# Up-projection tiles of two conv FFNs by seven block products on TensorE, with sums in place in PSUM

## Chip, core and metric

The program runs on one core of a Trainium2 chip. The metric is the device time of one execution in microseconds, where lower is better. All matrix products are made in three passes of float32r (a high and a low part of each operand), so that a product A·B is ah·bh + ah·bl + al·bh.

## What is computed

The reference is two layers of a diffusion backbone on 512 tokens of 1024 channels, with 256 tokens of context. Layer 0 is attention, layer 1 is Fourier mixing, and each ends with a gated feed-forward network with a depthwise convolution over three tokens. Cut to the part that the change touches:

```python
def conv_ffn(h, w_up, conv_w, conv_b, w_down):   # h: 512 x 1024, w_up: 1024 x 5632, w_down: 2816 x 1024
    u = h @ w_up                                  # gate and value, 2816 channels each
    u = depthwise_conv(u, conv_w) + conv_b        # taps at t-1, t, t+1, per channel
    gate, val = jnp.split(u, 2, axis=-1)
    return (silu(gate) * val) @ w_down
```

Around it stand RMS norms and adaLN: h = rms_norm(x) * (1 + scale) + shift, and x = x + gate * rms_norm(y). Scale, shift and gate come from products of the conditioning vector with 1024 x 6144 weights of each layer (the "adaLN sums" below).

## The kernel before

**Layout.** Channels are on partitions, tokens on the free axis: 8 channel tiles of x, 512 tokens, in two halves of 256. The modulated input of an FFN is held as `hh` and `hl` (high and low part, 8 x 512), the running output as `yT`.

**An FFN** (`ffn`, L974) works on 22 tiles `fi` of 128 gate channels and 128 value channels. For an ordinary tile the weights come by DMA (`raw`, 1 MB), are split into `wh` (a cast on ScalarE) and `wl` (a subtraction on VectorE), both by `split` at L113, and `up_mm` makes 8 x 3 matmuls of N=512 for the gate and as many for the value (`mm3`, L90 to L92). `conv` then takes the sums out of PSUM: one activation (L994) and two taps (L995, L997). `gated` makes silu (L1007), the product (L1008), and splits it into the pair `xh`, `xl`, the moving operand of the down-projection.

The first tiles (0 to 2, made of units u = 0 to 5) are different. They sweep over one half of the tokens while the other half's input is still being made (`begin`, `sweep`). In the second FFN the units' results still lack the tokens' norm factor R, which is multiplied in later at L993, with corrections of single columns (L1001). Meanwhile `remod` makes the real `hh` and `hl` (L216 to L223) for all later tiles.

**Groups.** `HALVES` splits the 22 tiles into 14 and 8. After a group its tiles are multiplied with their rows of `w_down` (`y_mm`), for 8 output tiles d. The first group's sums are copied to `yT` by ScalarE (L1100), the second's are added by VectorE (L1102). In the second group the first token half of all d goes first; then `mid` begins the next sub-layer for that half (norm sums at L170, R by L201, L204 and L205, the residual at L278 and L280, and for the Fourier part `hh` and `hl` at L332 and L333, squares summed by GpSimd at L339) while the second half's pass runs for d = 1 to 7. The squares of y of each half are summed by GpSimd (L253).

**Beside it.** The adaLN sums of layer 1 (`gemv_jobs`, L376 and L379, six jobs of five steps) run on VectorE in the first FFN, one step a tile and two an output tile of the first group (`GP = [1, 2]`).

**Order.** The tile framework schedules each engine's instructions into a fixed order at build time; an engine then works strictly in that order. Buffers come in rings: `raw` has three, `wh` and `wl` have four each, the accumulators `mm` have six banks of PSUM, `xh` and `xl` pairs (`Pairs`) have seven. SyncE issues the weight loads. `fence` and `held` keep some work behind other work.

## Time and profile before

| | us |
|---|---|
| Three runs | 1176.74, 1181.56, 1176.4 (median 1176.74) |
| Span of the profiled execution | 1176.5 |
| Busy: TensorE, VectorE, ScalarE, GpSimd | 1134.0, 751.6, 512.2, 201.1 |
| First FFN | about 340 to 703 |
| Fourier mixing | about 703 to 800 |
| Second FFN and the end | about 800 to 1176.5 |

The profile is taken from one execution. Its page gives busy times by engine, the chain of work that ended last and the costliest groups of instructions. Behind it the trace can be asked for groups by line and shape, for the table of windows, for the waits (an engine's idle time and who released it) and for the timeline. In a row of the timeline the first number is the start, the second the time until the last of its instructions ends, and brackets at the end give the idle time before it and its releaser. PE is TensorE (PEld its weight loads), DVE is VectorE, ACT is ScalarE, POOL is GpSimd. MATMUL ends are modelled and lie behind the start of the next; starts tell the pace.

### The profile page before, as it was taken

To read this page: it belongs to the slowest core of one execution; us is meant where nothing else is said; L and a number is where in the kernel's file an instruction comes from. 1 tells how busy PE (TensorE), PEld (TensorE's weight loads), DVE (VectorE), ACT (ScalarE), POOL (GpSimd) and SP (SyncE) were. 2 spreads that over 40 slices of the span, in tenths; PEclk is the share of its full clock that TensorE was granted. 3 is DMA by queue.
4 is the path that set the end of the run, shared out by engine and by line. 5 is a ranking of instruction groups with operands and counts; after the bars stand their busy time and mean duration, and the time that the engine had idled before them with its cause. 6 is when DMAs were issued, how large, how long until landed. Compare 5 with 4: busy or idle time off the path is not lost.

```text
span 1176.5 us, 17135 instructions
## 1 busy us (share of the span) xinstructions
PE 1134.0 (96%) x6878; PEld 946.1 (80%) x6878; DVE 751.6 (64%) x1215; ACT 512.2 (44%) x887; POOL 201.1 (17%) x213
## 2 busy tenths in 40 slices
PE   7999999999999999999999998988999999999995
PEld 4689898679898877777878998877788888888895
DVE  4673777675779685756665568988966532255555
ACT  3332356566554434322444445646644332234342
POOL 1132534222320000000000153663000000000013
PEclk9999999999999999999999999998999999999998
DMA  9432110874115353666622301621233222332112
GB/s 371 187 127 72 37 36 7 298 306 152 65 43 209 108 208 110 237 238 225 233 90 56 116 11 35 210 81 60 72 108 103 73 84 99 108 108 72 54 55 72
DMA packets 27127, 145.18 MB, mean 123 GB/s; under 512 B 2724, under 2 KB 7460, under 8 KB 14120
## 3 DMA queue, kind: packets, MB, share of 16 engines
q1 hardware_dynamic: 27048, 144.09, 35.0%
q8 instruction: 54, 0.88, 0.3%
q14 instruction: 25, 0.20, 0.1%
HBM read 141.98 MB, written 2.10 MB: 122 GB/s over the span
## 4 chain that ended last, share of the span: by engine, by line
PE 84%; DVE 11%; DMA 1%; ACT 1%; issue 1%; POOL 1%; SPq 0%; DVEq 0%; ACTq 0%; POOLq 0%
PE mm L90 24%; PE mm L92 23%; PE mm L91 23%; DVE md_t L278 2%; PE PT L786 2%; PE gm L405 1%; DVE hl L333 1%; PE O L90 1%; DVE wl L113 1%; DVE xT L280 1%; PE S L90 1%; PE O L91 1%; PE O L92 1%; PE S L92 1%; DMA xT<-in_xT 1%
## 5 line engine op out<-in xcount | busy, mean ns | idle before, releaser
L113 DVE TENSOR_TENSOR wl<-raw,wh 128x1024 fp32r<-128x1024 f32 (+1 forms) x139 | 167.6, 1210 | 207.8 <-ACT wh L113 207.5
L90 PE MATMUL mm<-hh,wh 128*128 128x512 f32 (+2 forms) x728 | 276.1, 379 | 0.0
L92 PE MATMUL mm<-hh,wl 128*128 128x512 f32 (+2 forms) x728 | 275.7, 379 | 0.0
L91 PE MATMUL mm<-hl,wh 128*128 128x512 f32 (+2 forms) x728 | 275.4, 378 | 0.0
L113 ACT CAST wh<-raw 128x1024 fp32r<-128x1024 f32 (+2 forms) x151 | 149.6, 999 | 183.4 <-PE mm L91 141.9
L90 PEld LDWEIGHTS mm<-hh,wh 128*128 128x128 f32 x728 | 137.7, 189 | 29.3 <-issue 1.2
L92 PEld LDWEIGHTS mm<-hh,wl 128*128 128x128 f32 x728 | 137.7, 189 | 27.9
L91 PEld LDWEIGHTS mm<-hl,wh 128*128 128x128 f32 x728 | 137.8, 189 | 27.5
L253 POOL TENSOR_TENSOR gacc<-gacc,sq 128x256 f32<-128x256 f32 (+1 forms) x35 | 31.5, 900 | 681.3 <-ACT sq L251 680.5
L90 PE MATMUL mm<-xh,wh 128*128 128x512 f32 (+1 forms) x368 | 131.5, 357 | 0.0
L91 PE MATMUL mm<-xl,wh 128*128 128x512 f32 (+1 forms) x368 | 130.6, 355 | 0.0
L92 PE MATMUL mm<-xh,wl 128*128 128x512 f32 (+1 forms) x368 | 130.5, 355 | 0.0
L90 PEld LDWEIGHTS mm<-xh,wh 128*128 128x128 f32 x368 | 69.2, 188 | 12.4 <-issue 1.2
L91 PEld LDWEIGHTS mm<-xl,wh 128*128 128x128 f32 x368 | 69.1, 188 | 11.1
L92 PEld LDWEIGHTS mm<-xh,wl 128*128 128x128 f32 x368 | 69.0, 187 | 11.0
L113 ACT CAST xh<-cv 128x512 fp32r<-128x512 f32 x44 | 27.3, 620 | 100.9 <-DVE cv L1008 100.9
L995 DVE SCALAR_TENSOR_TENSOR cv<-mm,cols,cv 128x511 f32<-128x511 f32 x83 | 61.8, 745 | 11.4 <-ACT cv L994 11.4
L994 ACT ACTIVATE cv<-mm,cols 128x512 f32<-128x512 f32 x83 | 64.2, 774 | 10.4 <-PE mm L92 10.4
L997 DVE SCALAR_TENSOR_TENSOR cv<-mm,cols,cv 128x511 f32<-128x511 f32 x83 | 62.2, 749 | 2.2
L1007 ACT ACTIVATE cv<-cv 128x512 f32<-128x512 f32 x44 | 27.8, 631 | 71.2 <-DVE cv L997 68.7
L379 DVE SCALAR_TENSOR_TENSOR gacc<-raw,scol,gacc 128x1024 f32<-128x1024 f32 x42 | 53.8, 1281 | 4.5 <-DMA raw<-in_mod_r 4.1
L91 PE MATMUL mm<-hl,xh 128*128 128x256 f32 (+1 forms) x160 | 47.3, 296 | 3.6 <-DVE hl L333 2.8
(358 smaller groups left out, 2238.7 us busy)
## 6 DMA issues: line engine op xcount, KB each, us to landing
raw<-in_w_up SPq DMA_DIRECT2D x44, 1024.0 KB, 5.0
raw<-in_mod_r SPq DMA_DIRECT2D x24, 1024.0 KB, 5.0
raw<-in_mod_p SPq DMA_DIRECT2D x16, 1024.0 KB, 6.4
raw<-in_w_down SPq DMA_DIRECT2D x16, 896.0 KB, 4.6
raw<-in_w_down SPq DMA_DIRECT2D x16, 512.0 KB, 3.7
raw<-in_w_in SPq DMA_DIRECT2D x6, 1024.0 KB, 5.0
raw<-in_w_out SPq DMA_DIRECT2D x4, 1024.0 KB, 6.0
raw<-in_w_f SPq DMA_DIRECT2D x8, 512.0 KB, 4.4
```

Of the source, the lines that this page charges most:

```text
L90: i = PE.matmul(out, lhsT=ah, rhs=bh, start=start, stop=False)
L91: PE.matmul(out, lhsT=ah, rhs=bl, start=False, stop=False)
L92: return i, PE.matmul(out, lhsT=al, rhs=bh, start=False, stop=stop)
L113: i = S.copy(out=h, in_=src), eng.tensor_tensor(out=l, in0=src, in1=f(h), op=ALU.subtract)
L253: G.tensor_tensor(out=self.acc[:, sl], in0=self.acc[:, sl], in1=sq[:, sl], op=ALU.add)
L278: m = V.scalar_tensor_tensor(out=t, in0=yT[:, k, hs], scalar=der[:, l, gi, k:k + 1], in1=R, op0=ALU.mult, op1=ALU.mult)
L379: held(V.scalar_tensor_tensor(out=acc, in0=w[:, i, :], scalar=scol[:, 0, k:k + 1], in1=acc, op0=ALU.mult, op1=ALU.add))
L786: PE.transpose(out=pt[:, j * P:(j + 1) * P], in_=Ps[j][:, off:off + P], identity=ident)
L994: S.activation(out=cv, in_=ps, func=AF.Identity, bias=bc, scale=wc[1])
L995: V.scalar_tensor_tensor(out=cv[:, 1:], in0=ps[:, :T - 1], scalar=wc[0], in1=cv[:, 1:], op0=ALU.mult, op1=ALU.add)
L997: V.scalar_tensor_tensor(out=cv[:, :T - 1], in0=ps[:, 1:], scalar=wc[2], in1=cv[:, :T - 1], op0=ALU.mult, op1=ALU.add)
L1007: S.activation(out=cg, in_=cg, func=AF.Silu)
```

## The change

In 6 tiles of the first FFN (4, 7, 10, 13, 16, 19) and 9 of the second (4, 6, ... 20) the up-projection is made by seven block products instead of eight. Channels are cut in two blocks of four tiles, tokens in two halves of 256, and the tile's outputs are gate and value: a 2 x 2 by 2 x 2 block product. Each of the seven is 4 x 3 matmuls of N=256.

- `seven_inputs`, once in each FFN, makes four sums of input blocks in `yT` on VectorE (L969 to L972) and splits them into four new pairs `zh`, `zl`. For this `remod` keeps the modulated float32 values in `yT`, with one more ScalarE operation for every second channel tile (`kept`).
- `seven_weights`, for each tile, makes four sums of weight blocks on VectorE (L984, L986, L987, in a buffer of the `raw` ring) and four splits: "1" of 512 columns, "57", "63" and "24" of 1024.
- `seven_products` uses two accumulators x and y. Sums of products that are needed in two places are copied by ScalarE (L1017, L1019, L1022, L1027, 128x256) and added by VectorE in place in PSUM (L1025, L1028, 128x512). The value comes out negated, so the convolution takes negated taps (`ncw`).
- The 22 tiles form three groups of 8, 8 and 6. Groups two and three are added to `yT` by VectorE. In every group the first two output tiles are begun with all but the last channel tile. `w_down` of a group comes in one split for each output tile.
- The ring of `wh` and `wl` has five buffers, the ring of `xh` and `xl` pairs four, beside the four `zh`, `zl`. In the last group output tiles 4 to 6 take theirs from `zh`, `zl`.
- The adaLN sums take one step at an ordinary tile, none at a seven-product tile, and one at an output tile of the first two groups. The last of the six jobs moves into the second FFN.

Line numbers of the changed kernel differ: `split` is L118, `mm3` is L95 to L97, the conv's lines are L1075 (product with R), L1076, L1077, L1079 and L1083, `gated` is L1089 and L1090, the remodulation L221 to L229, the adaLN step L390, the norm sums' matmuls L175 and L360, GpSimd's adds L263, L290 and L350, the group sums L1191 and L1193.

```diff
-HALVES = [(0, 14), (14, 8)]
+GROUPS = [(0, 8), (8, 8), (16, 6)]
+FIRST = 3
+SEVEN = [range(4, NF, 3), range(4, NF, 2)]
-GP = [1, 2]
+GP = [1, 1]
...
     def wpair(shape):
-        return mk(wp, shape, F32R, "wh", 4), mk(wp, shape, F32R, "wl", 4)
+        return mk(wp, shape, F32R, "wh", 5), mk(wp, shape, F32R, "wl", 5)
...
-    def mod_tiles(items, R):
+    def mod_tiles(items, R, kept=None):
         for i, (h, l, src, am, bm) in enumerate(items):
-            t = mk(cp, [P, HT], F32, "md_t", 4)
-            if i % 2:
+            t = mk(cp, [P, HT], F32, "md_t", 4) if kept is None else kept[i]
+            if kept is not None and i % 2 == 0:
+                V.scalar_tensor_tensor(out=t, in0=src, scalar=am, in1=R, op0=ALU.mult, op1=ALU.mult)
+                S.activation(out=t, in_=t, func=AF.Identity, bias=bm, scale=1.0)
+                S.copy(out=h, in_=t)
+                V.tensor_tensor(out=l, in0=t, in1=f(h), op=ALU.subtract)
+            elif i % 2:
...
+    def seven_inputs(xp):
+        (b11, b12), (b21, b22) = blocks_of(yT)
+        hi, lo = blocks_of(hh), blocks_of(hl)
+        V.tensor_tensor(out=b11, in0=b11, in1=b12, op=ALU.subtract)
+        V.tensor_tensor(out=b12, in0=b22, in1=b12, op=ALU.subtract)
+        V.scalar_tensor_tensor(out=b22, in0=b22, scalar=-1.0, in1=b11, op0=ALU.mult, op1=ALU.subtract)
+        V.scalar_tensor_tensor(out=b21, in0=b22, scalar=-1.0, in1=b21, op0=ALU.mult, op1=ALU.subtract)
+        b = {"1": (hi[0][0], lo[0][0]), "2": (hi[1][0], lo[1][0]), "3": (hi[1][1], lo[1][1])}
+        for n, src in (("5", b11), ("6", b22), ("4", b21), ("7", b12)):
+            b[n] = xp.spare([P, KH, HT])
+            split(*b[n], src)
+        return b
+
+    def seven_weights(l, fi):
+        r = raw([P, 2, KC, P], a["w_up"][l, fi])
+        s = mk(wp, [P, 4, KH, P], F32, "raw", 3)
+        a4 = r.rearrange("p i (c k) n -> p (i c) k n", c=2)
+        V.tensor_tensor(out=s[:, 0:2], in0=a4[:, 3::-3], in1=a4[:, 2].unsqueeze(1).to_broadcast([P, 2, KH, P]),
+                        op=ALU.add)
+        V.tensor_tensor(out=s[:, 2], in0=s[:, 0], in1=a4[:, 0], op=ALU.add)
+        V.tensor_tensor(out=s[:, 3], in0=s[:, 2], in1=a4[:, 1], op=ALU.add)
+        w = {}
+        for names, src in (("1", a4[:, 0:1]), ("57", s[:, 0:2]), ("63", s[:, 2:4]), ("24", a4[:, 1::2])):
+            wh, wl = wpair([P, len(names), KH, P])
+            split(wh, wl, src)
+            for i, n in enumerate(names):
+                w[n] = wh[:, i], wl[:, i]
+        return w
...
+        product("1", y, 1)
+        S.copy(out=xs[:, :HT], in_=y[:, HT:])
+        product("5", x, 1)
+        S.copy(out=ys[:, HT:], in_=x[:, HT:])
+        product("2", x, 0)
+        product("6", y, 1)
+        S.copy(out=xs[:, HT:], in_=y[:, HT:])
+        product("4", y, 0)
+        product("3", x, 1)
+        V.tensor_tensor(out=x, in0=x, in1=xs, op=ALU.add)
+        product("7", y, 1)
+        S.copy(out=ys[:, :HT], in_=y[:, HT:])
+        V.tensor_tensor(out=y, in0=y, in1=ys, op=ALU.add)
+        return x, y
...
-        for hf, (f0, nch) in enumerate(HALVES):
-            for fi in range(max(f0, 3), f0 + nch):
+        bs = seven_inputs(xp)
...
+        for gi, (f0, nch) in enumerate(GROUPS):
+            end = gi == len(GROUPS) - 1
+            for fi in range(max(f0, FIRST), f0 + nch):
+                if fi in SEVEN[l]:
+                    cc = [conv(fi, i, u, None, i == 1) for i, u in enumerate(seven_products(l, fi, pps, bs))]
...
-                if gem is not None:
+                if gem is not None and fi not in SEVEN[l]:
                     pump(gem, GP[0])
...
-                if hf == 0:
+                if gi == 0:
                     S.copy(out=yT[:, d, sl], in_=ps[:, sl])
                 else:
                     V.tensor_tensor(out=yT[:, d, sl], in0=yT[:, d, sl], in1=ps[:, sl], op=ALU.add)
+                if end:
                     ys.add(pps, yT[:, d, sl], hs)
...
-                 gemv_jobs([(1, v) for v in range(6)], pps))
+                 gemv_jobs([(1, v) for v in range(5)], pps))
...
-                 lambda y: pump(boundary(y, 0, 1, 3, pps, None, a["out"]), 100), None, plain)
+                 lambda y: pump(boundary(y, 0, 1, 3, pps, None, a["out"]), 100), gemv_jobs([(1, 5)], pps), plain)
```

**VectorE, second FFN, around the beginning of tile 4.** Before, the convs of tiles 2 (cv of mm_1202), 3 (mm_1268, mm_1272) and 4 (mm_1277) stand here, with the split of tile 5's value weights (wl_1291) and the gates' splits (xl):

```order
L995 SCALAR_TENSOR_TENSOR cv1_1262_8183<-mm_1202_7739,cols_1_61,cv1_1262_8183 128x511
L113 TENSOR_TENSOR wl_1291_8375<-raw_1285_8339,wh_1290_8374 128x1024
L113 TENSOR_TENSOR xl_1255_8101<-cv1_1258_8113,xh_1254_8100 128x512
L997 SCALAR_TENSOR_TENSOR cv1_1262_8183<-mm_1202_7739,cols_1_61,cv1_1262_8183 128x511
L995 SCALAR_TENSOR_TENSOR cv0_1269_8224<-mm_1268_8199,cols_1_61,cv0_1269_8224 128x511
L1008 TENSOR_TENSOR cv1_1262_8183<-cv0_1260_8126,cv1_1262_8183 128x512
L997 SCALAR_TENSOR_TENSOR cv0_1269_8224<-mm_1268_8199,cols_1_61,cv0_1269_8224 128x511
L995 SCALAR_TENSOR_TENSOR cv1_1273_8257<-mm_1272_8232,cols_1_61,cv1_1273_8257 128x511
L113 TENSOR_TENSOR xl_1264_8190<-cv1_1262_8183,xh_1263_8189 128x512
```

Now, behind the same tile 2 (cv1_1289): the last input sum, four splits zl of the input sums, tile 3's taps (mm_1304, mm_1308), and tile 4's splits of the weights "63" (wl_1319) and "24" (wl_1321):

```order
L972 SCALAR_TENSOR_TENSOR yT_4_65<-yT_4_65 128x4x256
L1090 TENSOR_TENSOR cv1_1289_8486<-cv0_1287_8429,cv1_1289_8486 128x512
L118 TENSOR_TENSOR zl_1293_8501<-yT_4_65,zh_1292_8500 128x1024
L118 TENSOR_TENSOR xl_1291_8493<-cv1_1289_8486,xh_1290_8492 128x512
L118 TENSOR_TENSOR zl_1295_8505<-yT_4_65,zh_1294_8504 128x1024
L118 TENSOR_TENSOR zl_1297_8509<-yT_4_65,zh_1296_8508 128x1024
L118 TENSOR_TENSOR zl_1299_8513<-yT_4_65,zh_1298_8512 128x1024
L1077 SCALAR_TENSOR_TENSOR cv0_1305_8549<-mm_1304_8524,cols_1_61,cv0_1305_8549 128x511
L1077 SCALAR_TENSOR_TENSOR cv1_1309_8582<-mm_1308_8557,cols_1_61,cv1_1309_8582 128x511
L118 TENSOR_TENSOR wl_1319_8610<-raw_1313_8597,wh_1318_8609 128x1024
L1090 TENSOR_TENSOR cv1_1309_8582<-cv0_1305_8549,cv1_1309_8582 128x512
L118 TENSOR_TENSOR wl_1321_8614<-raw_1312_8595,wh_1320_8613 128x1024
```

Tile 4's operands were split well ahead of this place before (its wl_1276 and wl_1280); now they stand in it, behind the input sums.

**TensorE at the same place.** Before, the last matmuls of tile 3 (mm_1272) and the first of tile 4 (mm_1277):

```order
L91 MATMUL mm_1272_8232<-hl_6_67,wh_1270_8228 128x512
L92 MATMUL mm_1272_8232<-hh_5_66,wl_1271_8229 128x512
L90 MATMUL mm_1277_8271<-hh_5_66,wh_1275_8267 128x512
L91 MATMUL mm_1277_8271<-hl_6_67,wh_1275_8267 128x512
L92 MATMUL mm_1277_8271<-hh_5_66,wl_1276_8268 128x512
```

Now tile 4 is made of products (mm_1323 is y, mm_1322 is x; wh_1314 is "1", wh_1316 "57", wh_1318 "63"), with four matmuls of tile 5 (mm_1333, mm_1337) between them:

```order
L97 MATMUL mm_1323_8618<-hh_5_66,wl_1315_8602 128x256
L95 MATMUL mm_1322_8617<-zh_1292_8500,wh_1316_8605 128x256
L95 MATMUL mm_1333_8731<-hh_5_66,wh_1331_8727 128x512
L96 MATMUL mm_1333_8731<-hl_6_67,wh_1331_8727 128x512
L95 MATMUL mm_1323_8618<-zh_1294_8504,wh_1318_8609 128x256
L95 MATMUL mm_1337_8764<-hh_5_66,wh_1335_8760 128x512
L96 MATMUL mm_1337_8764<-hl_6_67,wh_1335_8760 128x512
L96 MATMUL mm_1322_8617<-zl_1293_8501,wh_1316_8605 128x256
L97 MATMUL mm_1322_8617<-zh_1292_8500,wl_1317_8606 128x256
```

The second matmul of product 5 needs zl_1293, and everything of TensorE stands behind it in this order.

**TensorE in a later seven-product tile of the second FFN** (tile 10: mm_1442 is y, mm_1441 is x; the ordinary tile there before reads like the rows above): product 6 has four matmuls between product 5 and product 2.

```order
L97 MATMUL mm_1441_9503<-zh_1292_8500,wl_1436_9492 128x256
L95 MATMUL mm_1442_9504<-zh_1294_8504,wh_1437_9495 128x256
L96 MATMUL mm_1442_9504<-zl_1295_8505,wh_1437_9495 128x256
L97 MATMUL mm_1442_9504<-zh_1294_8504,wl_1438_9496 128x256
L95 MATMUL mm_1442_9504<-zh_1294_8504,wh_1437_9495 128x256
L95 MATMUL mm_1441_9503<-hh_5_66,wh_1439_9499 128x256
L96 MATMUL mm_1441_9503<-hl_6_67,wh_1439_9499 128x256
```

Product 2 (on wh_1439) goes into the first half of the bank whose second half product 5 has just filled.

95 lines of the change are left out of this document (57 added, 38 removed).

## The prediction

> **What bounds the kernel now.** I read the page first, for the busy shares and the chain.
>
> ```profile
> span 1176.5 us, 17135 instructions
> PE 1134.0 (96%) x6878; PEld 946.1 (80%) x6878; DVE 751.6 (64%) x1215; ACT 512.2 (44%) x887; POOL 201.1 (17%) x213
> PE 84%; DVE 11%; DMA 1%; ACT 1%; issue 1%; POOL 1%; SPq 0%; DVEq 0%; ACTq 0%; POOLq 0%
> ```
>
> TensorE is busy for 96% of the span and 84% of the chain is on it. So the matmul stream decides, as long as it is fed. Whether it is fed is a question of the stage, so next came the table of windows (busy time with the number of instructions; then clock, DMA share, GB/s).
>
> ```profile
> 350.00:450.00 100.00, 100.00 (x464) 81.21 (x463) 77.12 (x92) 43.95 (x58) 0.00 (x0) 1.00 0.48 168
> 806.00:856.00 50.00, 47.93 (x276) 40.63 (x275) 48.13 (x89) 34.75 (x58) 6.89 (x8) 1.00 0.22 70
> 860.00:960.00 100.00, 100.00 (x428) 80.35 (x427) 58.15 (x71) 40.24 (x52) 0.00 (x0) 1.00 0.26 89
> ```
>
> In the middle of both FFNs (first and third row) PE never stops, at full clock. VectorE has room there: 77 of 100 us where it carries the adaLN sums, 58 of 100 in the second FFN. The second row is the beginning of the second FFN: there VectorE works 48.13 of 50 us. What is added to VectorE is free in the third row's place and has no room in the second's.
>
> **What a seven-product tile gains on PE.** An ordinary tile is 48 matmuls of N=512, a seven-product tile 7 x 12 = 84 of N=256. The pitch of each comes from the timeline: the first and the last row of 171 steps at N=512, and of 143 steps at N=256 (the first matmul of the next kind ends those).
>
> ```profile
> 859.80 0.39 PE L91 MATMUL mm<-hl,wh 128*128 128x512 f32 x1
> 899.87 0.39 PE L91 MATMUL mm<-hl,wh 128*128 128x512 f32 x1
> ...
> 339.79 0.28 PE L91 MATMUL mm<-hl,wh 128*128 128x256 f32 x1
> 356.88 0.40 PE L90 MATMUL mm<-hh,wh 128*128 128x512 f32 x1
> ```
>
> 40.07/171 = 0.2343 us and 17.09/143 = 0.1195 us. A tile goes from 48 x 0.2343 = 11.25 us to 84 x 0.1195 = 10.04 us, a gain of 1.21 us. There are 6 such tiles in the first FFN and 9 in the second: 15 x 1.21 = 18.1 us at most. That is 11% of a tile, not the 1/8 of the products, as two matmuls of N=256 take a little longer than one of N=512.
>
> The Trainium skill speaks against this: "TensorE: Matmul & The Clock Gate", section "Back-to-back issue gap", gives a sustained pace of about 81 ns at N=128 and 131 ns at N=512, because each matmul's weight load counts too. Between these, an estimate for N=256 is 98 ns, and 84 x 98 ns would be 1.9 us more than 48 x 131 ns: 15 tiles would lose 29 us instead of gaining 18. The trace disagrees with both figures; its rows halve with N, so I go by the rows.
>
> **What it costs on the other engines.** The rows that price it, VectorE first, grouped by form over the FFNs (columns: sum, mean ns; then idle before):
>
> ```profile
> L113 DVE TENSOR_TENSOR wl<-raw,wh 128x1024 fp32r<-128x1024 f32 x86 | 105.6, 1231 | 121.0 <-ACT wh L113 120.8
> L995 DVE SCALAR_TENSOR_TENSOR cv<-mm,cols,cv 128x511 f32<-128x511 f32 x83 | 61.8, 745 | 11.4 <-ACT cv L994 11.4
> L379 DVE SCALAR_TENSOR_TENSOR gacc<-raw,scol,gacc 128x1024 f32<-128x1024 f32 x42 | 53.8, 1281 | 4.5 <-DMA raw<-in_mod_r 4.1
> L1008 DVE TENSOR_TENSOR cv<-cv,cv 128x512 f32<-128x512 f32 x44 | 30.4, 691 | 1.2
> L1102 DVE TENSOR_TENSOR yT<-yT,mm 128x512 f32<-128x512 f32 x2 | 1.4, 679 | 0.0
> L205 ACT COPY Rs<-misc 128x256 f32<-128x256 f32 x6 | 2.2, 370 | 12.8 <-PE misc L204 12.8
> ```
>
> On VectorE a seven-product tile takes 1.23 + 2 x 0.69 for the weights' sums, 3 x 1.23 + 0.69 for four splits (3.5 widths of 1024 instead of 2), 2 x 0.68 for the sums in PSUM, 4 x 0.745 for the convolution and 2 x 0.69 for the gate: 12.7 us, against 6.8 us of an ordinary tile (2 x 1.23 + 4 x 0.745 + 2 x 0.69). Beside each other, as in the second FFN, 19.5 us stand against 10.04 + 11.25 = 21.3 us of PE. So VectorE keeps up, and I put nothing down for it in the steady parts. Of the pattern one seven, two ordinary with an adaLN step each (2 x 1.28) in the first FFN: 12.7 + 2 x 9.4 = 31.5 against 32.5 us. That only just fits.
>
> **A wait inside each seven-product tile.** The second half of a bank is copied by ScalarE before the first half is written. In the changed order product 2 stands only four matmuls of product 6 behind product 5, and waits for the copy of product 5's sums. A matmul of N=256 is recorded with 0.28 us, 0.16 beyond its pitch. The copy is 0.37 us (L205 above); the steps from engine to engine are 0.04 and 0.15 us:
>
> ```profile
> 686.53 0.67 PE L204 MATMUL misc<-Rs,con 128*128 128x256 f32 x2 [1.05 <-DVE Rs L201]
> 687.24 0.37 ACT L205 COPY Rs<-misc 128x256 f32<-128x256 f32 x1 [2.57 <-PE misc L204]
> ...
> 685.00 1.38 DVE L201 TENSOR_TENSOR Rs<-st_v,con 128x256 f32<-128x256 f32 x1
> ```
>
> (687.24 less 687.20; 686.53 less 686.38.) 0.16 + 0.04 + 0.37 + 0.15 = 0.72 us, less 4 x 0.1195 = 0.48: 0.2 us a tile, 15 x 0.2 = 3 us. Product 4 waits likewise for product 6's copy, but with eight matmuls (0.96 us) between. Bounds: 0 if the copy is seen earlier, 0.7 if both are missed. That the two halves of one bank can't be used apart is what the Trainium skill states in "PSUM — Partial Sum Buffer", section "Terms": two engines on the same bank and quadrant at once are a collision. No run here shows one.
>
> **The first seven-product tile of the second FFN** is the largest loss. VectorE there, before the change:
>
> ```profile
> 826.42 0.42 DVE L219 TENSOR_TENSOR hl<-md_t,hh 128x256 fp32r<-128x256 f32 x1
> 834.81 1.41 DVE L995 SCALAR_TENSOR_TENSOR cv<-sq,cols,cv 128x511 f32<-128x511 f32 x2
> 836.13 0.75 DVE L997 SCALAR_TENSOR_TENSOR cv<-sq,cols,cv 128x511 f32<-128x511 f32 x1
> 837.74 0.69 DVE L1008 TENSOR_TENSOR cv<-cv,cv 128x512 f32<-128x512 f32 x1
> 838.34 0.75 DVE L995 SCALAR_TENSOR_TENSOR cv<-mm,cols,cv 128x511 f32<-128x511 f32 x1
> 839.00 1.22 DVE L113 TENSOR_TENSOR wl<-raw,wh 128x1024 fp32r<-128x1024 f32 x1
> 840.13 0.69 DVE L113 TENSOR_TENSOR xl<-cv,xh 128x512 fp32r<-128x512 f32 x1
> 848.64 0.75 DVE L995 SCALAR_TENSOR_TENSOR cv<-mm,cols,cv 128x511 f32<-128x511 f32 x1 [1.40 <-ACT cv L994]
> ```
>
> It runs without a gap until 847.2, and starts follow each other closer than the recorded durations: 0.66 for a tap, 0.60 for 128x512, 1.13 for 128x1024. Tile 4 starts on PE at 836.4 and tile 5 ends at 858.9, which the activations that follow them show (847.84 is the end of tile 4: less 11.25, plus 11.25):
>
> ```profile
> 847.84 0.77 ACT L994 ACTIVATE cv<-mm,cols 128x512 f32<-128x512 f32 x1
> 859.08 0.78 ACT L994 ACTIVATE cv<-mm,cols 128x512 f32<-128x512 f32 x1
> ```
>
> In the new order, the last remodulated tile comes 1 us later (827.9 against 826.84): two sums L969 and L970 of about 1.13 us stand ahead of it, less what moved behind it. From there to the split wl_1321 VectorE has 16 taps (16 x 0.66), 6 products with R (0.33 each), 10 single columns (0.08), L971 and L972 (1.28 each), 4 gates and 3 splits of 128x512 (7 x 0.60) and 6 splits of 128x1024 (6 x 1.13): 10.6 + 2.0 + 0.8 + 2.6 + 4.2 + 6.8 = 27.0 us, to 854.9. PE has tile 4's first product ready (837.4 to 838.8), then four matmuls of tile 5, and needs zl_1293 (845), wl_1319 (853.1) and wl_1321 (854.9). 49 of the 84 matmuls are left then: 5.9 us, to 860.8; 44 matmuls of tile 5, 10.3 us, to 871.1. Against 858.9 that is **12.2 us later**, the tile's own gain and the 1 us of the remodulation counted in. The bounds are 0 (all operands in time, -0.2) and 14 (every row at its recorded duration). I take 12.2, since the order is fixed and each row is priced from this place.
>
> **The end of the first FFN.** The last group has 6 channel tiles instead of 8. Its second pass of 7 output tiles shrinks by 7 x 6 x 0.1195 = 5.0 us, done earlier instead. But the work meanwhile on the first half does not shrink:
>
> ```profile
> 680.51 0.42 DVE L1102 TENSOR_TENSOR yT<-yT,mm 128x256 f32<-128x256 f32 x1 [2.40 <-PE mm L92]
> ...
> 701.67 5.63 POOL L253 TENSOR_TENSOR gacc<-gacc,sq 128x256 f32<-128x256 f32 x6 [0.36 <-ACT sq L251]
> 702.75 0.95 PE L349 MATMUL misc<-ones,yT 128*128 128x2 f32 x8
> ...
> 707.36 0.42 PE L170 MATMUL misc<-gacc,ones 128*32 128x64 f32 x8 [2.13 <-POOL gacc L253]
> ```
>
> From the first half's end (680.5) to GpSimd's last sum (707.3) there are 26.8 us, and PE already waits 2.13 us for it. In the new order the six sums stand behind the same adds on GpSimd. So the 5.0 us are lost here (bounds 2 to 5). At the kernel's end the same shortening costs nothing that I count:
>
> ```profile
> 1142.15 0.42 DVE L1102 TENSOR_TENSOR yT<-yT,mm 128x256 f32<-128x256 f32 x1 [2.40 <-PE mm L92]
> ...
> 1154.07 0.85 POOL L280 TENSOR_TENSOR xT<-xT,md_t 128x256 f32<-128x256 f32 x1 [0.76 <-DVE md_t L278]
> 1155.25 2.38 POOL L253 TENSOR_TENSOR gacc<-gacc,sq 128x256 f32<-128x256 f32 x3 [0.33 <-ACT sq L251]
> ```
>
> There GpSimd has four sums of 0.79 us left at 1154.9 in the new order and is done at 1158.1; PE's pass of 7 x 18 x 0.1195 = 15.1 us, which begins about 1142.6, ends at 1157.7.
>
> Smaller: the first seven-product tile of the first FFN gets its last splits about 1 us late (0 to 4; the 97% above). The two channel tiles that now go at N=512 in one pass save 7 x 2 x 3 x (2 x 0.1195 - 0.2343) = 0.2 us an FFN. The new group's two output tiles begun early are 2 x 7 x 3 x 0.234 = 9.8 us, more than the last tile's way to its split: an activation, two taps, silu, gate, cast, split, with the three on ScalarE at 0.77, 0.77 x 3 + 0.66 x 2 + 0.60 x 2 = 4.8 us.
>
> **The sum.** First FFN: 6 x (-1.21 + 0.2) + 1 + 5.0 - 0.2 = -0.3. Second: 12.2 + 8 x (-1.21 + 0.2) - 0.2 = +3.9. Together +3.6 on the span of 1176.5, which lies 0.2 under the median of 1176.74: **1180 us**. About 0.5% (6 us) is what a measurement of this kernel can tell from no change.
>
> **Rivals.**
> - *The gain stays.* The first seven-product tile of the second FFN isn't starved, because VectorE finds its operands early and gets ahead in the 3 us it waits for R before 806. Then 12.2 becomes -1.0 + 1: 1180 - 12.2 = 1168. For: 58% load later. Against: no gap from 806.4 to 847. Chance 0.20.
> - *Slower, by ScalarE's queue.* Product 4 waits for product 6's copy (L1022), which stands behind the cast of the preceding tile's gate (xh), which waits for VectorE's product (L1090). That cast ends about 5.1 us into a tile (activation 0.8, VectorE from 1.9 on after a weight cast of about 1.1, split 1.13, tap 0.66, gate 0.60, cast 0.77), and 48 + 8 matmuls and the 0.2 us put product 4 at 6.9, so the copy may begin at 6.4. If VectorE is over 1.3 us later than that, PE waits in each tile; 1 us more in 14 tiles gives 1194. For: 19.5 of 21.3 us leaves 1.8. Against: starts are closer than durations, so 18 of 21.3. Chance 0.17.
> - *Weight loads set the pace.* A load of 128 columns is recorded with 0.189 us:
>
> ```profile
> L90 PEld LDWEIGHTS mm<-hh,wh 128*128 128x128 f32 x728 | 137.7, 189 | 29.3 <-issue 1.2
> ```
>
> If loads could not overlap further at N=256, a tile would take 84 x 0.189 = 15.9 us, 15 x 4.6 = 69 us more than now, 1180 + 18 + 69 = 1267. The 143 steps at 0.1195 speak against it. Chance 0.02.
>
> **How the numbers follow.** My own case has 0.61, from 1171 to 1188 by the bounds of its terms; 0.43 of it is within 0.5% (1170.9 to 1182.6) and 0.18 above. With the rivals: faster 0.20, same 0.43, slower 0.37. The range is 1167 to 1193: it takes in most of the first rival and half of the second.
>
> **What would show it.** Right: PE's timeline has some 13 us of idle in the first seven-product tile of the second FFN, waiting for zl and wl on VectorE; 4 to 7 us ahead of L360 or L175 at the first FFN's end; short gaps of 0.2 us behind four matmuls in every seven-product tile; 84 matmuls 0.12 apart. Wrong: gaps in every pair on L1022 or on wl, a pitch over 0.125, or no gap at that first tile.

## The result, and the profile after the change

The changed kernel takes 1186.91 us (median of 10 runs, 1184.98 to 1189.71) against 1179.41 us of the kernel before in the same session (10 runs, 1176.4 to 1184.12). The ratio is 1.006, with a 95% interval of 1.0043 to 1.0077. It is some 7 us slower than before and 7 us above the forecast of 1180, inside the forecast range; the interval lies on the border between "same" and "slower by over 0.5%". The forecast started from 1176.74 us, the median of three runs, which is 2.7 below the median of the session; as a change, 3.6 us were forecast and about 7.1 measured, twice as much. The profiled execution has a span of 1185.6 us, 9.1 more than the one before, and the ledger below is made against that. Both profiles stand at the same time when the first FFN begins (copy of R at 332.98 before, 333.05 now).

The page of the changed kernel, the lines that answer to the first fence of the prediction:

```profile
span 1185.6 us, 18362 instructions
PE 1124.2 (95%) x7334; PEld 961.1 (81%) x7334; DVE 851.7 (72%) x1354; ACT 565.2 (48%) x1001; POOL 198.9 (17%) x213
PE 79%; DVE 13%; POOL 2%; ACT 2%; DMA 1%; issue 1%; SPq 0%; DVEq 0%; POOLq 0%; ACTq 0%
```

PE is busy for 9.8 us less: products are saved, though less busy time than the 18.1 us of the prediction, in part because some of the work goes at half clock (below). VectorE works 100 us more, and its share of the chain goes from 11 to 13%, PE's from 84 to 79%. What is saved is waited away. Where, the table of windows shows (busy time with the number of instructions, then clock, DMA share, GB/s):

```profile
350.00:450.00 100.00, 98.90 (x541) 83.89 (x540) 82.97 (x97) 47.10 (x67) 0.00 (x0) 1.00 0.51 179
806.00:860.00 54.00, 40.09 (x227) 35.18 (x227) 51.65 (x91) 35.85 (x65) 7.52 (x8) 0.85 0.13 42
860.00:960.00 100.00, 100.00 (x531) 84.21 (x531) 64.72 (x76) 43.88 (x64) 0.00 (x0) 1.00 0.39 136
```

The middles of both FFNs are about as full as before (98.90 and 100.00 of 100 us). The beginning of the second FFN is not: PE was busy 47.93 of 50 us there and is now busy 40.09 of 54, at a mean clock of 0.85. These are PE's waits in that place, from its timeline (a row's bracket has the idle time and what ended it):

```profile
822.10 0.38 PE L95 MATMUL mm<-hh,xh 128*128 128x256 f32 x1 [2.72 <-ACT hh L223]
823.15 0.58 PE L96 MATMUL mm<-hl,xh 128*128 128x256 f32 x1 [0.67 <-DVE hl L224]
843.06 0.39 PE L95 MATMUL mm<-zh,wh 128*128 128x256 f32 x1 [2.25 <-ACT sq L1017]
844.48 0.76 PE L95 MATMUL mm<-hh,wh 128*128 128x512 f32 x1 [1.04 <-DVE cv L1083]
847.33 0.58 PE L96 MATMUL mm<-zl,wh 128*128 128x256 f32 x1 [1.66 <-DVE zl L118]
850.51 0.39 PE L95 MATMUL mm<-hh,wh 128*128 128x256 f32 x1 [0.25 <-ACT sq L1019]
855.10 0.58 PE L97 MATMUL mm<-zh,wl 128*128 128x256 f32 x1 [4.09 <-DVE wl L118]
```

The first two, 3.4 us, stand behind the last copy of R (818.00), where PE waits for the remodulated hh and hl. The other five, 9.3 us, lie in the tile that the prediction named, but only 5.75 us of them are for the operands that it named (zl and wl). 2.25 us are for ScalarE's copy of product 1's sums, and 1.04 for a convolution on VectorE. Behind the waits comes something the prediction did not name. The same table in stretches of 2 us, the clock third from the right:

```profile
844.00:846.00 2.00, 1.19 (x2) 0.50 (x2) 2.00 (x4) 1.58 (x3) 0.00 (x0) 0.50 0.00 0
848.00:850.00 2.00, 2.00 (x11) 1.96 (x10) 2.00 (x2) 0.09 (x1) 0.00 (x0) 0.50 0.00 0
856.00:858.00 2.00, 2.00 (x10) 1.83 (x10) 2.00 (x3) 0.31 (x1) 0.00 (x0) 0.50 0.85 270
858.00:860.00 2.00, 2.00 (x12) 2.00 (x11) 1.65 (x2) 0.00 (x0) 0.00 (x0) 0.50 0.99 315
862.00:864.00 2.00, 2.00 (x19) 2.00 (x18) 1.53 (x2) 0.00 (x0) 0.00 (x0) 1.00 0.47 139
```

After the longer waits the granted clock is 0.50: in the stretches that PE fills, 10 to 12 matmuls of N=256 start in 2 us instead of 19. From 855.10 on there are 56 matmuls of N=256 and 44 of N=512 until tile 5 ends, 17.0 us at the paces of the prediction, and they take 19.5 (until 874.64). So half clock adds 2.5 us behind the last wait alone.

The rest of the kernel by milestones, all from the two profiles:

| Place | before | after | shift | the step from the line above |
|---|---|---|---|---|
| First FFN's end: PE at the norm sums (L170, now L175) | 707.36 | 704.07 | −3.3 | −3.3 |
| Fourier's end: copy of R (L205, now L210) | 773.11 | 772.55 | −0.6 | +2.7 |
| Second FFN: the last copy of R | 817.30 | 818.00 | +0.7 | +1.3 |
| Tile 5 of the second FFN ends | 858.87 | 874.64 | +15.8 | +15.1 |
| First half's end of the second FFN | 1142.15 | 1155.78 | +13.6 | −2.1 |
| End | 1176.5 | 1185.6 | +9.1 | −4.5 |

### The profile page after: what moved, and what is told of

Same layout as the page of the kernel before. It is cut to its first block, busy times and chain, and to the rows that moved or that the text cites. A ratio compares the mean times of both kernels' runs of the same rounds, so it can differ in the third digit from the quotient of the medians.

```text
span 1185.6 us, 18362 instructions
## 1 busy us (share of the span) xinstructions
PE 1124.2 (95%) x7334; PEld 961.1 (81%) x7334; DVE 851.7 (72%) x1354; ACT 565.2 (48%) x1001; POOL 198.9 (17%) x213
## 4 chain that ended last, share of the span: by engine, by line
PE 79%; DVE 13%; POOL 2%; ACT 2%; DMA 1%; issue 1%; SPq 0%; DVEq 0%; POOLq 0%; ACTq 0%
PE mm L95 22%; PE mm L97 21%; PE mm L96 21%; DVE md_t L288 2%; PE PT L797 2%; PE gm L416 1%; DVE hl L344 1%; DVE wl L118 1%; PE O L95 1%; DVE xT L290 1%; PE S L95 1%; PE O L96 1%; DVE yT L221 1%; PE S L97 1%; PE gm L95 1%
## 5 line engine op out<-in xcount | busy, mean ns | idle before, releaser
L118 DVE TENSOR_TENSOR wl<-raw,wh 128x1024 fp32r<-128x1024 f32 (+2 forms) x169 | 194.6, 1160 | 102.5 <-ACT wh L118 101.8
L118 ACT CAST wh<-raw 128x1024 fp32r<-128x1024 f32 (+2 forms) x181 | 174.6, 978 | 190.8 <-PE mm L96 98.6
L95 PE MATMUL mm<-hh,wh 128*128 128x512 f32 (+2 forms) x668 | 233.2, 349 | 1.4 <-DVE cv L1083 1.0
L96 PE MATMUL mm<-hl,wh 128*128 128x512 f32 (+2 forms) x668 | 231.8, 347 | 0.1
L97 PE MATMUL mm<-hh,wl 128*128 128x512 f32 (+2 forms) x668 | 231.0, 346 | 0.0
L263 POOL TENSOR_TENSOR gacc<-gacc,sq 128x256 f32<-128x256 f32 (+1 forms) x35 | 30.6, 875 | 696.7 <-ACT sq L261 695.7
L95 PEld LDWEIGHTS mm<-hh,wh 128*128 128x128 f32 x668 | 127.1, 190 | 20.2 <-ACT sq L1019 1.4
L97 PEld LDWEIGHTS mm<-hh,wl 128*128 128x128 f32 x668 | 126.9, 190 | 16.7 <-DVE wl L118 0.2
L95 PE MATMUL mm<-xh,wh 128*128 128x512 f32 (+1 forms) x364 | 133.6, 367 | 0.0
L97 PE MATMUL mm<-xh,wl 128*128 128x512 f32 (+1 forms) x364 | 132.8, 365 | 0.0
L95 PEld LDWEIGHTS mm<-xh,wh 128*128 128x128 f32 x364 | 68.5, 188 | 13.7 <-issue 1.6
L97 PEld LDWEIGHTS mm<-xh,wl 128*128 128x128 f32 x364 | 68.4, 188 | 12.1
L97 PE MATMUL mm<-zh,wl 128*128 128x256 f32 x240 | 68.1, 284 | 5.2 <-DVE wl L118 5.2
L95 PE MATMUL mm<-zh,wh 128*128 128x256 f32 x240 | 70.0, 291 | 2.2 <-ACT sq L1017 2.2
L96 PE MATMUL mm<-zl,wh 128*128 128x256 f32 x240 | 68.1, 284 | 1.7 <-DVE zl L118 1.7
L1076 ACT ACTIVATE cv<-mm,cols 128x512 f32<-128x512 f32 x68 | 52.7, 775 | 29.1 <-PE mm L97 23.3
L1077 DVE SCALAR_TENSOR_TENSOR cv<-mm,cols,cv 128x511 f32<-128x511 f32 x68 | 50.5, 745 | 13.3 <-ACT cv L1076 13.2
L1193 DVE TENSOR_TENSOR yT<-yT,mm 128x256 f32<-128x256 f32 (+1 forms) x46 | 23.5, 522 | 48.2 <-PE mm L97 48.2
L390 DVE SCALAR_TENSOR_TENSOR gacc<-raw,scol,gacc 128x1024 f32<-128x1024 f32 x42 | 53.8, 1282 | 6.0 <-DMA raw<-in_mod_r 5.5
```

The costliest lines, as they stand in the source:

```text
L95: i = PE.matmul(out, lhsT=ah, rhs=bh, start=start, stop=False, skip_group_check=skip)
L96: PE.matmul(out, lhsT=ah, rhs=bl, start=False, stop=False, skip_group_check=skip)
L97: return i, PE.matmul(out, lhsT=al, rhs=bh, start=False, stop=stop, skip_group_check=skip)
L118: i = S.copy(out=h, in_=src), eng.tensor_tensor(out=l, in0=src, in1=f(h), op=ALU.subtract)
L263: G.tensor_tensor(out=self.acc[:, sl], in0=self.acc[:, sl], in1=sq[:, sl], op=ALU.add)
L390: held(V.scalar_tensor_tensor(out=acc, in0=w[:, i, :], scalar=scol[:, 0, k:k + 1], in1=acc, op0=ALU.mult, op1=ALU.add))
```

## Experiments

The question is what makes the 15 us between the last copy of R in the second FFN and the end of tile 5, and whether the prediction's reason holds: the first seven-product tile needs operands that VectorE makes too late. Since profiles differ by some us in what lies ahead (the copy of R that opens the first FFN stands between 331.2 and 336.9 us), they are compared by one distance that all have: from the last copy of R (L210 or L205) to the activation of tile 7's value. Tile 7 is an ordinary tile in all of them and, except in the kernel before with its group of 14, the last before the first down-projection. Each distance is read from one profiled execution.

| Kernel | second FFN | last copy of R | tile 7's value | distance |
|---|---|---|---|---|
| before | as before | 817.30 | 881.58 | 64.3 |
| changed | inputs in front, tiles 4 and 6 seven products | 818.00 | 896.39 | 78.4 |
| e1 | inputs in front, tile 6 seven products | 819.26 | 896.75 | 77.5 |
| e4 | as changed, PE kept running in tile 4 | 820.65 | 898.26 | 77.6 |
| e5 | inputs asked for later, not pinned | 821.83 | 896.89 | 75.1 |
| e6 | inputs in front, all ordinary | 821.72 | 900.08 | 78.4 |
| e7 | no inputs, remodulation as before | 818.49 | 882.10 | 63.6 |
| e8 | as e7 | 824.97 | 888.38 | 63.4 |
| e10 | no inputs, remodulation kept | 817.81 | 884.64 | 66.8 |
| e9 | inputs pinned behind tile 5 | 818.49 | 884.23 | 65.7 |

### e1: the first seven-product tile later

```diff
-SEVEN = [range(4, NF, 3), range(4, NF, 2)]
+SEVEN = [range(4, NF, 3), range(6, NF, 2)]
```

> The second FFN's seven-product tiles begin with tile 6 instead of 4 (8 tiles instead of 9). Theory (the loss sits in the first such tile there, where VectorE is behind and TensorE stands still): TensorE has two ordinary tiles more to cover VectorE's input sums and splits, so tile 5 ends at most 3 us later than before the change instead of 15.8; the one tile less gives back 1 us. Span 14 us shorter than the changed kernel's, about 1171 to 1173; ratio to the kernel before 0.995 to 0.998. Rival (seven-product tiles are slow everywhere): one of 15 is gone, the time moves by less than 1 us, ratio 1.006.

Measured: 1187.96 us, ratio to before 1.0065 (1.004 to 1.0089), span 1185.6. The time is the rival's and not the theory's: nothing was gained. But the trace doesn't show a loss in every tile, as the rival has it. The stall moved to where PE goes through ordinary tile 5 (the first row is a matmul of tile 6 that stands ahead), and nearly kept its size, 8.3 us:

```profile
856.16 0.36 PE L95 MATMUL mm<-hh,wh 128*128 128x256 f32 x1 [3.23 <-DVE cv L1079]
861.69 0.80 PE L97 MATMUL mm<-hh,wl 128*128 128x512 f32 x1 [5.06 <-DVE wl L118]
```

So the prediction's place was right and its reason too narrow. The longer wait here is for weights of an ordinary tile: VectorE is late for whatever comes next, and not only for a seven-product tile's own operands. I took up the theory that the input work (`seven_inputs`, four sums and four splits, 9.3 us) is VectorE's backlog in a stretch without room.

### e2: the group of six in the middle

```diff
-GROUPS = [(0, 8), (8, 8), (16, 6)]
+GROUPS = [(0, 8), (8, 6), (14, 8)]
```

> Groups of 8, 6 and 8 tiles instead of 8, 8 and 6, all else as changed: the last group's second pass has its 20 us again. Theory (the first FFN's end is bound by the other half's work, so a shorter pass is lost): 4 to 6 us shorter than the changed kernel, ratio to before about 1.001. Rival (the pass has nothing to do with it): ratio 1.006 as before, within 0.001.

Measured: 1185.85 us, ratio 1.0039 (1.002 to 1.0057), span 1184.1. That is some 2.5 us better by the ratios, about half of what was expected. The wait at L175 shrinks from 3.10 to 1.11 us. Counted from the copy of R that opens the first FFN (334.75 here, 333.05 in the changed kernel), the two copies of R at its end (681.98 and 704.46) come 4.6 and 5.5 us earlier, as the theory had it, but the next milestone, 771.23, only 3.0. On the way stands this stretch:

```profile
758.00:760.00 2.00, 0.86 (x8) 0.65 (x6) 2.00 (x2) 2.00 (x3) 1.94 (x2) 1.00 0.68 143
760.00:762.00 2.00, 1.34 (x7) 1.34 (x8) 1.70 (x4) 0.55 (x3) 2.00 (x1) 0.70 0.82 340
762.00:764.00 2.00, 2.00 (x9) 1.55 (x8) 0.42 (x1) 1.25 (x4) 2.00 (x2) 0.50 0.32 131
764.00:766.00 2.00, 2.00 (x9) 2.00 (x10) 0.00 (x0) 0.00 (x0) 2.00 (x2) 0.50 0.00 0
766.00:768.00 2.00, 1.83 (x37) 1.41 (x35) 0.42 (x1) 0.15 (x1) 0.38 (x1) 0.59 0.90 266
```

A row of PE's timeline ends the idle time at its beginning:

```profile
760.66 0.47 PE L97 MATMUL mm<-B,wl 128*128 128x256 f32 x1 [1.80 <-DVE wl L118]
```

One wait of 1.80 us is followed by some 6.5 us at half clock. The Fourier part, from the copy at 704.46 to the one at 771.23, takes 66.8 us instead of 64.3, and that eats the rest.

### e3: GpSimd's weight splits behind its last sum of the Fourier part

The Fourier part became 2.7 us longer, which no step of the prediction had. GpSimd now made both weight splits of the second FFN's tile 1 ahead of the last sum `acc`, for which PE waits at L175 (before, one split stood ahead and one behind):

```profile
760.69 5.70 POOL L118 TENSOR_TENSOR wl<-raw,wh 128x1024 fp32r<-128x1024 f32 x2
766.36 1.25 POOL L263 TENSOR_TENSOR acc<-acc,sq 128x512 f32<-128x512 f32 x1
```

```diff
+                self.g = G.tensor_tensor(out=self.acc[:, sl], in0=self.acc[:, sl], in1=sq[:, sl], op=ALU.add)
...
+        fences[y1.g.ins.engine] = y1.g.ins.name
         early += up_weights(1, wpair, [1], G)
```

> Only GpSimd's order at the end of the Fourier part is changed: the two weight splits of the second FFN's tile 1 stand behind the last sum of squares instead of ahead of it, as one of them did before the change. Theory (the 2.17 us wait of TensorE on that sum, and the half clock after it, are what the Fourier part lost): 2 to 3 us shorter than the changed kernel, ratio 1.004. Rival (the splits are then late themselves): no change or up to 3 us longer.

Measured: 1186.6 us, ratio 1.0057 (1.0038 to 1.0076): no difference from the changed kernel that can be told. GpSimd's wait is gone, and from one copy of R to the next (706.91 to 770.08) it is 63.2 us instead of 64.3 (before the change 61.4), but later waits for Rs come in or grow: 1.60 us at 769.37, and 2.12 us at 814.73 where it was 1.24. A large part of what was removed is waited for elsewhere.

### e4: PE kept running through the stall

```diff
+    def keep_up(pps, after, n):
+        ps = mk(pps, [P, T], F32, "misc", 2)
+        for _ in range(n):
+            i = PE.matmul(ps[:32, :256], lhsT=ones32, rhs=con[:, :256], start=True, stop=True)
+            follow(i, after)
+            after = i
+        return after
```

Eight such products stand behind product 1 of tile 4 and fourteen behind the first matmul of product 2.

> 22 small matmuls that nothing reads are put into TensorE's two idle stretches in the first seven-product tile of the second FFN, 8 behind product 1 and 14 behind product 2's first matmul. Theory (after idling TensorE runs at half clock for some 5 us, which costs 2 to 3.5 us here on top of the wait): the matmuls behind the last wait go at 0.12 instead of 0.21 us, and the span is 2 to 3 us shorter than the changed kernel's, ratio 1.004. Rival (all of it is VectorE's lateness): no change, or longer by up to 1 us where the small matmuls overrun.

Measured: 1187.51 us, ratio 1.0058 (1.0036 to 1.0079). No gain. The timeline tells why:

```profile
853.69 6.23 PE L1000 MATMUL misc<-con,ones 128*32 128x256 f32 x28
859.85 0.39 PE L97 MATMUL mm<-zh,wl 128*128 128x256 f32 x1
860.07 0.28 PE L95 MATMUL mm<-zh,wh 128*128 128x256 f32 x1
860.19 0.28 PE L96 MATMUL mm<-zl,wh 128*128 128x256 f32 x1
```

From the second on, the matmuls behind the last stretch are 0.12 us apart, instead of 0.21 in the changed kernel: where the idle time is filled, the clock is 1.00 (from 854 on; 0.54 to 0.60 from 850 to 854, behind a wait of 2.15 us that stayed). But the fourteen fillers, plain float32, are recorded as 28 and take 6.23 us, 0.44 us each; they run until 859.85, while the split they were to bridge ended at 857.69. What the clock gave, 2.2 us of overrun took. So the pitch shows the mechanism; a net gain was not shown.

### e5: the inputs asked for one step a tile

`seven_inputs` becomes a generator of four steps, called at tiles 4 to 7, and the seven-product tiles of the second FFN start at 8.

```diff
+                for _ in range(4 if (l, fi) == (0, FIRST) else l == 1 and 4 <= fi < 8):
+                    bs = next(inputs)
```

> The input sums and splits of the second FFN are made one step a tile at tiles 4 to 7, and its seven-product tiles are 8, 10, ... 20 (7 instead of 9; the first FFN is unchanged). Theory (VectorE's backlog at the start of the second FFN, made by the 9.3 us of input sums and splits, is what PE waits for, whichever tile needs them first): from the last copy of R (L210) to the start of tile 5's end PE is back to about 42 us (41.6 before the change, 56.6 with it), no wait over 2 us, and the span is some 12 us under the changed kernel's (14 less of stall, 2 more for two seven-product tiles fewer): about 1174, ratio to before 0.995 to 1.000. Rival (the seven-product tiles need more of VectorE than there is anywhere in the second FFN): the waits come back at tiles 8 to 12, ratio 1.004 or more.

Measured: 1187.12 us, ratio 1.0053 (1.0035 to 1.0072). Missed by both: neither is the stall gone nor does it come back at tiles 8 to 12. PE has one long wait, 6.78 us at tile 5 (862.94, for wl). VectorE's timeline shows that the call had moved and the work only in part:

```profile
827.15 1.21 DVE L969 TENSOR_TENSOR yT<-yT 128x1024 f32<-128x1024 f32 x1
...
835.69 1.21 DVE L970 TENSOR_TENSOR yT<-yT 128x1024 f32<-128x1024 f32 x1
...
844.51 0.69 DVE L1090 TENSOR_TENSOR cv<-cv,cv 128x512 f32<-128x512 f32 x1 [2.82 <-ACT cv L1089]
```

The framework sorts what is ready by its own rules, so two of the four sums still ran in the full stretch, and the others at 853.30 and 855.03, still ahead of tile 5's wl. The last row is a second effect: VectorE, though late, waits 2.82 us for a silu. ScalarE's timeline has the reason:

```profile
842.89 1.05 ACT L118 CAST wh<-raw 128x1024 fp32r<-128x1024 f32 x1 [3.72 <-PE mm L96]
843.85 0.63 ACT L1089 ACTIVATE cv<-cv 128x512 f32<-128x512 f32 x1
```

The silu stands behind the cast of a weight for which there is no free buffer in the ring until PE is done with an older one. The Trainium skill states that ScalarE and VectorE take their instructions strictly in order ("TensorE: Matmul & The Clock Gate", section "Architectural detail: the array is 16× 32×32, not 1× 128×128"); these rows agree.

### e6, e7, e8: the parts one by one

e6 leaves the inputs where they are and has no seven-product tile in the second FFN; e7 leaves out the inputs and the kept remodulation there as well; e8 has no seven-product tile in either FFN.

```diff
-SEVEN = [range(4, NF, 3), range(4, NF, 2)]
+SEVEN = [range(4, NF, 3), ()]
...
-        bs = seven_inputs(xp)
+        bs = seven_inputs(xp) if l == 0 else None
```

(e6 has the first change, e7 both and `kept` only in the first FFN, e8 empty ranges in both.)

> The second FFN makes its input sums and their splits as in the changed kernel but has only ordinary tiles, so nothing there uses them; the first FFN is unchanged. Backlog theory: the 9.3 us of input work alone, put where VectorE has some 8.8 us in hand (tile 5's wl was split at 839.0 and needed at 847.8), makes PE wait 2 to 6 us before tile 6; from R's copy to tile 6's start 43.5 to 47.5 us. Rival (the wait belongs to the seven-product tile 4 alone): 41.6 to 42.5 us. The end: as e7_ffn1_only plus that wait.

> No seven-product tile and no input sums in the second FFN; first FFN, three groups and rings as changed. Both theories: from R's copy to tile 6's start 41.6 us as before the change; the end at the changed kernel's less the 14 to 15 us of stall and plus the 8 to 9 us that nine seven-product tiles gained: about 6 us under it, ratio to before 1.000 to 1.003. If the ledger is wrong and a part of the second FFN's loss is the groups' or the adaLN job's, the time from R's copy to tile 6's start stays over 44.

> No seven-product tile at all, no input sums and no kept copies; three groups of 8, 8 and 6, the rings and the moved adaLN job as changed. From the ledger of the changed kernel's profile less its seven-product tiles (5 at 1.0 us and one wait of 1.1 in the first FFN): first FFN's end (PE at the norm sums' L175) about 1.5 us later than before, Fourier part 2.8 us longer, tile 6 of the second FFN 4 us later, the end 5 us later: ratio 1.003 to 1.006. Rival (the groups cost nothing, all of the loss is the seven-product tiles'): ratio 0.999 to 1.001.

Measured: e6 1193.92 us, ratio 1.0116 (1.0085 to 1.0148); e7 1178.58, 0.9991 (0.9974 to 1.0008); e8 1185.28, 1.0038 (1.0019 to 1.0057). PE's waits behind the last copy of R in e6:

```profile
824.59 0.58 PE L95 MATMUL mm<-hh,xh 128*128 128x256 f32 x1 [2.10 <-ACT hh L223]
826.50 0.58 PE L96 MATMUL mm<-hl,xh 128*128 128x256 f32 x1 [1.34 <-DVE hl L224]
859.46 0.47 PE L95 MATMUL mm<-hh,wh 128*128 128x512 f32 x1 [4.00 <-DVE cv L1079]
864.99 0.80 PE L97 MATMUL mm<-hh,wl 128*128 128x512 f32 x1 [3.68 <-DVE wl L118]
```

In e6 nothing uses the inputs, and yet the distance is 78.4 us, as long as in the changed kernel. e7, without them, has 63.6. So preparing the inputs (keeping, summing and splitting them) makes a loss of this size without any seven-product tile. That tiles 4 and 6 as seven products leave the distance as it is means that they don't bring their 2 us there either. I had expected 2 to 6 us for the inputs and it is 14.8: VectorE's time in hand was overestimated, a wait of VectorE for a silu (3.21 us at 844.79) stands in the stretch too, and the clock is 0.50 from 860 to 870.

e8 shows that the three groups, with their rings and the moved adaLN job, cost 4.2 us (1185.28 against 1181.08 in that session; 0.2 to 0.6% by the interval), as expected. e8 less e7 is what the six seven-product tiles of the first FFN bring, with their inputs: 5.6 us by the ratios. In the traces it is 3.7 us, from the copy of R that opens the first FFN to the one at its end (380.2 and 376.5).

### e9, e10: the inputs pinned behind tile 5; the kept remodulation alone

In e9 the first sum is ordered behind the gate product of tile 5 on VectorE, and the seven-product tiles start at 8. In e10 the second FFN keeps the float32 values in yT but makes no inputs.

```diff
+                if (l, fi) == (1, 6):
+                    bs = seven_inputs(xp, gs["v"])
...
+        if after is not None:
+            follow(i, after)
```

> The input sums and splits of the second FFN are pinned on VectorE behind the gate product of tile 5, which e5 had only asked for without pinning (there two of the four sums still ran at 827 and 836); seven-product tiles 8, 10, ... 20; the kept form of the remodulation stays. Theory (what PE waits for after the start of the second FFN is VectorE's 9.3 us of input work in the stretch from R's copy to tile 6): PE's waits from R's copy to the first group's down-projection add up to under 4 us (e6: 13 us, e7: 2.4), and the span is 11 to 13 us under the changed kernel's: about 1174, ratio 0.994 to 0.999. Rival (the kept form of the remodulation, with one more ScalarE operation for every second tile and a weight cast ahead of a silu, is what starves VectorE): 6 us of waits or more stay, ratio 1.001 or more.

> As e7 (no seven-product tile and no input sums in the second FFN), but the remodulation there keeps its float32 values in yT as in the changed kernel. The output is the reference's. Theory of the input work: within 2 us of e7 (span about 1178 to 1179.5, PE waits from R's copy on up to 2 us more than e7's 2.4). Rival (the kept form): 5 us or more over e7.

Measured: e9 1176.63 us, ratio 0.9977 (0.9964 to 0.9991), span 1173.5. e10 1183.19, 1.0034 (1.0017 to 1.0051), span 1179.7. The sums in e9, and the windows of the stretch in e9 and in the kernel before:

```profile
866.99 1.22 DVE L969 TENSOR_TENSOR yT<-yT 128x1024 f32<-128x1024 f32 x1
...
876.68 2.35 DVE L118 TENSOR_TENSOR zl<-yT,zh 128x1024 fp32r<-128x1024 f32 x2
```

```profile
826.00:882.00 56.00, 56.00 (x247) 45.77 (x246) 52.43 (x81) 32.36 (x43) 0.00 (x0) 0.98 0.25 85
```

```profile
826.00:882.00 56.00, 56.00 (x244) 45.20 (x243) 42.97 (x71) 30.18 (x42) 0.00 (x0) 1.00 0.28 95
```

VectorE is busy for 52.43 us against 42.97 (the inputs, and adaLN steps that moved here), and PE does not wait at all. e6 and e9 have the same instructions up to tile 7, at another place, and it costs 13 us less: the distance is 65.7 instead of 78.4. That settles the cause of the larger part. The waits from the copy of R on are 2.8 us, all of them ahead of 824 and like those of e10, which has no inputs: 66.8 against 63.6 of e7, 3.2 us that belong to the kept form of the remodulation. There PE waits for hh and hl (1.75 and 1.34 us in e10, 0.19 and 0.15 in e7). By this distance the kept form costs more than the 2 us of the theory and less than the 5 of the rival. The times leave the rival room: e10 lies 0.43% above e7 by the ratios, some 5 us, from two sessions and with intervals of 0.17% to either side. So the kept form is a second cause, of 3 to 5 us, beside the place of the sums and splits.

### e11, e12: what it can bring, and where VectorE ends

e11 is e9 with the groups of e2 and the order of e3. e12 is e9 with all tiles from 8 on as seven products.

```diff
+SEVEN = [range(4, NF, 3), range(8, NF)]
```

> e9 with groups of 8, 6 and 8 (e2) and GpSimd's weight splits behind the last acc sum (e3). If the effects add: 2.5 us of e2 and about 1 of e3 off e9: about 1171, ratio 0.990 to 0.996, and so the first version under the kernel before. If the pass at the first FFN's end only moves the wait on, as in e3: like e9.

> e9 with every tile from 8 on as seven products (14 in the second FFN instead of 7). If VectorE needs the 11.7 to 12.7 us a tile that the prediction priced, consecutive seven-product tiles go at that pace instead of 10.24, and the kernel is 5 to 14 us slower than e9. If VectorE keeps up (it can work ahead in the down-projections), they go at 10.24 and it is 6 us faster than e9.

Measured: e11 1171.53 us against 1179.41, ratio 0.9939 (0.9919 to 0.9959), span 1169.5: 0.6% faster than the kernel before and the version here that beats it most clearly (e9's interval, too, lies below 1). e12 1187.22, 1.0065 (1.0041 to 1.009), 10.6 us slower than e9. In e12 VectorE and PE stand like this, where e9 had PE busy without a gap, and PE waits in the tiles that follow each other:

```profile
940.00:1027.00 87.00, 81.11 (x624) 76.84 (x623) 83.55 (x108) 56.03 (x91) 0.00 (x0) 0.98 0.29 98
```

```profile
976.26 0.39 PE L97 MATMUL mm<-hh,wl 128*128 128x256 f32 x1 [1.98 <-DVE wl L118]
981.63 0.39 PE L95 MATMUL mm<-hh,wh 128*128 128x256 f32 x1 [0.52 <-ACT sq L1021]
```

VectorE works 83.55 of 87 us. From the last tile of the first group to the last of the second it is 140.8 us (885.55 to 1026.32) against 132.1 in e9 (884.23 to 1016.30). Less the same down-projection, 132.1 − 4 x 10.24 − 4 x 11.2 = 46.3, eight seven-product tiles take 94.5 us, 11.8 each: close to the 11.7 to 12.7 us of VectorE in the expectation, not PE's 10.24. VectorE feeds every second tile, and not every tile; nothing between was run.

## Why the prediction came out as it did

**The sum.** The time lies in the range, but the ledger has 9.1 us where the sum had 3.6. The first seven-product tile of the second FFN costs 15.1 us there instead of 12.2; the Fourier part 2.7 and the way from there to the last copy of R 1.3, where it had nothing; the rest of the second FFN gains 6.6 instead of 8.3. Against this the first FFN is 3.3 us shorter, not 0.3. That this last miss nearly cancels the Fourier part's is luck. The 1.3 us are not traced further.

**The tile.** Right. The seven-product tiles of the second FFN behind the first take 10.24 us in the mean (10.08 to 10.38), ordinary ones 11.2: the 10.04 + 0.2 of the prediction. No pitch by weight loads: 0.118 to 0.12 us. e9 and e10, of one session, show the gain in the time: seven such tiles, and inputs that cost little where they stand, bring 6.6 us (1176.63 for 1183.19), where 7 x 1.01 = 7.1 was the price. The runs also decide against the prediction's estimate from the Trainium skill ("TensorE: Matmul & The Clock Gate", section "Back-to-back issue gap"), by which fifteen tiles would have lost 29 us: e7, with six such tiles, is faster than e8 with none.

**The wait inside the tile.** Right in kind. In a tile of the second FFN the step ahead of product 2 is 0.26 us, and product 2 starts right behind the copy of product 5 (877.97 + 0.38):

```profile
878.14 0.28 PE L95 MATMUL mm<-zh,wh 128*128 128x256 f32 x1
878.40 0.39 PE L95 MATMUL mm<-hh,wh 128*128 128x256 f32 x1
...
877.97 0.38 ACT L1019 COPY sq<-mm 128x256 f32<-128x256 f32 x1
```

A like step stands ahead of product 4 (880.86 to 881.12), where none was expected.

**ScalarE's queue as the slower rival.** Not in the steady parts: behind tile 5 of the second FFN PE has no wait for L1022 up to 1150. ScalarE's order does hurt at the beginning. There a weight cast that waits for PE stands ahead of a silu (e5), and in the changed kernel VectorE waits for such a silu, and PE for the copy of product 1's sums. That product's last matmul starts at 839.95, and ScalarE comes to the copy at 842.64:

```profile
840.22 0.69 DVE L1090 TENSOR_TENSOR cv<-cv,cv 128x512 f32<-128x512 f32 x1 [2.00 <-ACT cv L1089]
842.64 0.36 ACT L1017 COPY sq<-mm 128x256 f32<-128x256 f32 x1
```

**The first seven-product tile of the second FFN, 12.2 us.** This is the step that was mis-sized, and its reason was too narrow. From the last copy of R to the end of tile 5 it is 15.1 us more. PE is idle for 12.7 us of it (0.4 before), but the 13 forecast were to stand in the tile, for zl and wl. 5.75 us stand there for these two, 3.5 there for ScalarE's copies and a convolution, and 3.4 ahead of the tile for hh and hl. The remaining 2.8 us are lost while PE works, although its work is shorter. Operands: zl came at 847.3 and not 845, wl_1319 at 855.1 and not 853.1, since VectorE, which I took as never idle, had to wait 2.00 us for a silu at 840.22. Clock: 2.5 us behind the last wait, which I did not have at all. Reason: I charged it to the tile that needs the operands first; e1 and e6 show that it is the input work, with or without a user. And the remodulation was put down with 1 us. The first tap behind it came as forecast (827.95 for 827.9), but the kept form costs 3.2 us until tile 7 (e10): PE waits for hh and hl directly, a wait that the sum did not have.

**The ends of the FFNs.** The 5.0 us lost at the end of the first were right in place, and the size is open within the bounds of 2 to 5. PE waits at L360 and L175:

```profile
698.11 1.05 PE L360 MATMUL misc<-ones,yT 128*128 128x2 f32 x8 [2.34 <-POOL yT L350]
704.07 0.44 PE L175 MATMUL misc<-gacc,ones 128*32 128x64 f32 x8 [3.10 <-POOL gacc L263]
```

That is 3.3 us more than the 2.13 before. e2 takes 5.5 us off the first FFN, by its last copy of R. e8, which has the groups alone, needs only 1.4 us more than before from the first FFN's opening copy of R to its last (336.49 to 716.69, before 332.98 to 711.74), or about 2.4 without the adaLN job that moved out. The first FFN's end is 3.3 us earlier where I had 0.3. About 1.0 of that is PE work of this job (matmuls behind its L384 and L390 come 0.77 and 0.22 us late in the kernel before), which is paid again in the second FFN; the other 2 us are not traced. The kernel's end keeps 4.5 of the 5.0 us, as forecast.

**The Fourier part, +2.7 us.** No step of mine had it. I followed the queues of PE, VectorE and ScalarE past the moved code, and not GpSimd's, where a second split of 2.85 us had moved ahead of a sum that PE waits for. e3 shows that the wait can go; it does not show that the time comes back with it, so a part of these 2.7 us stays unexplained.

**The first seven-product tile of the first FFN, 1 us.** Right: 1.09 us, at 370.78.
